# Split weights and split activations at changing byte offsets in a two-layer decoder kernel

## The chip, the cores and the metric

The kernel runs on one core of a Trainium2 chip. The time is the device time of one execution, in microseconds; the kernel before takes 2146.15 us (median of three runs, 2145.81 to 2146.16). A profile is one further execution of the same program, taken by the hardware profiler. Engines are called as the profile calls them: PE multiplies matrices (PEld is its loading of the stationary operand), DVE, ACT and POOL work elementwise, SP issues DMAs.

## The reference

Two decoder layers on 256 tokens of 2048 channels, in float32. Layer 0 mixes with a diagonal state-space model (S5) and a gated linear unit, layer 1 with windowed attention; a SwiGLU feed-forward follows each.

```python
def reference(x, ...):
    h = x
    for i in range(DEPTH):
        hn = rmsnorm(h, norm_mix[i])
        if i % N_MIXERS == 0:
            mix = s5_mixer(hn, ...)          # ends in gl = gelu(y) @ w_glu ; a * sigmoid(b)
        else:
            mix = sliding_window_attention(hn, w_qkv, b_qkv, sinks, w_o)
        h = h + mix
        hn = rmsnorm(h, norm_ffn[i])
        h = h + swiglu(hn, w_gate[i], w_up[i], w_down[i])
    return rmsnorm(h, norm_final)

def swiglu(x, w_gate, w_up, w_down):
    return (jax.nn.silu(x @ w_gate) * (x @ w_up)) @ w_down
```

Nearly all of the arithmetic is in the products with the seven weight matrices (w_glu, w_qkv, w_o, and gate, up and down twice).

## The kernel before

**Pieces.** Every weight matrix is cut into pieces of 512 rows by 512 columns, 332 in all, listed in the order of use. SP loads a piece (1 MB) into one of two `raw` buffers. ACT copies it, rounded, into the first half of a buffer `w` (L120, the high part), and DVE writes the difference `raw - high` into the second half (L121, the low part). A `w` tile is [128 partitions, 2 parts, 4 groups of channels, 512 columns], 16384 bytes on each partition.

**Three places for `w`.** `place` gives them out in turns: two buffers of the pool `wq`, allocated at the kernel's start (here: the first and the second place), and one of the pool `wp`, allocated after S5 (the third place; every third piece). While PE uses piece i, `next` has pieces up to i+2 split and up to i+4 loaded.

**Activations** are split in the same way: a tile holds [128, 2 parts, 4 groups of channels, 256 tokens], 8192 bytes on each partition. `turned_tile` (pool `pp`, four buffers) gives `gt` (the input of the gated unit), `hT` (the hidden part of SwiGLU) and `oT` (the attention's output). `normed_tile` (pool `wp`, four buffers) gives `xT`, the normalised h.

**The products.** `piece` runs 24 steps on PE for each piece of weights: 4 groups of channels, 2 halves of the tokens, and 3 products, high by high (L734), high activations by low weights (L735), low activations by high weights (L736). In each step the activations are the stationary operand (128 columns, 512 bytes on a partition, read by the weight load) and the weights the moving operand (512 columns, 2048 bytes). That makes 332 x 24 = 7968 steps. Between two pieces PE may do small work that was left for it (transposes, the attention's scores).

**Where the parts start.** Every stride inside these tiles is a multiple of 512 bytes, so that what a start address leaves modulo 512 is the same for all 24 steps of a piece. From the built program:

| tiles | pool | start modulo 512 bytes |
|---|---|---|
| `w`, first and second place | `wq` | 320 |
| `w`, third place | `wp` | 384 |
| `gt`, `hT`, `oT` | `pp` | 320 |
| `xT` | `wp` | 384 |

The *distance* of a piece is, in all that follows, the start of its activations minus the start of its weights, modulo 512 bytes. There are three distances: 0, 64 and 448. Of the 332 pieces 155 are at 0 (65 in the third place with `xT`, 46 in the second and 44 in the first place with a tile of `pp`), 131 at 64 (first or second place with `xT`) and 46 at 448 (third place with a tile of `pp`).

**Order.** The order on each engine is made by a scheduler when the program is built; instructions under `pin` or `tc.keep_in_program_order` stay where they are written. A buffer's reuse waits for the last reader of what it held.

Of the kernel before, what the change touches and what calls it, by code (L numbers as in the profile page):

```python
# [9 lines left out]
F32 = mybir.dt.float32  # L10
# [7 lines left out]
P = 128  # L18
D = 2048
# [27 lines left out]
def bc(ap, axis, n):  # L47
    """`ap` with a repeated axis of n put in."""
    v = ap.unsqueeze(axis)
    shape = list(v.shape)  # L50
    shape[axis] = n
    return v.to_broadcast(shape)
# [3 lines left out]
def kernel(  # L56
# [25 lines left out]
    # parts of activations, channels on partitions: [channel, high/low, 128 channels, token]  # L82
    def turned_tile(name):
        return pp.tile([P, 2, 4, T], F32R, tag="b8", name=nm(name))

    def normed_tile(name):
        return wp.tile([P, 2, 4, T], F32R, tag="xt", name=nm(name), bufs=4)

# [1 line left out]
    class Weights:  # L90
# [18 lines left out]
        def place(self, i):  # L109
            """in turns, but for the first the third place isn't there yet"""  # L110
            pool, n = (wp, 1) if i % 3 == 0 and i > 0 else (wq, 2)
            return pool.tile([P, 2, 4, 512], F32R, tag="w", name=nm("w"), bufs=n)
# [50 lines left out]
    # the last heads come while the first two chunks of the outputs have what the others give  # L163
# [12 lines left out]
    # work that an earlier product left for the tensor engine, done between a later one's pieces  # L176
    left = []
    # the same, a list for each of the next pieces
    slots = []

# [1 line left out]
    def s5():  # L182
        st = ExitStack()
        with st:
# [8 lines left out]
            def pin(ins):  # L193
                """in this place among its engine's work"""
                return tc.keep_in_program_order(ins)
# [7 lines left out]
            # the states; until then, room for what does not stay  # L203
# [4 lines left out]
            # loads  # L208
# [34 lines left out]
            # masks: row (j, g2, c) belongs to g2 = 0 / 1 ; sign of the re / im half  # L243
# [11 lines left out]
            def lay(nat):  # L255
                """banks of [(re/im, state), channel, group]"""
                pts = [bank([P, 4, G]) for _ in range(GC // 4)]
                for c in range(GC):
                    PE.transpose(pts[c // 4][:, c % 4], nat(c), ident)
                return pts  # L260

            def laid(pts, name, sign):
                """[(re/im, state), group, channel], times a sign per partition"""
                o = big([P, G, GC], name)
                for i, pt in enumerate(pts):
                    pin(S.activation(o[:, :, 4 * i : 4 * i + 4], pt.rearrange("p c g -> p g c"), AF.Copy, scale=sign))
                return o

            # the norm of x: rows' sums of squares
# [11 lines left out]
            # the norm's weights go into B (and D)  # L281
# [5 lines left out]
            # the other norms' weights, channels on partitions  # L287
# [4 lines left out]
            # parameters, [group, state]  # L292
# [42 lines left out]
            # powers of lambda: [group, power - 1, re/im, state]  # L335
# [5 lines left out]
            def cmul(o, a, b, n):  # L341
                """o = a * b, complex, [G, n, 2, NS]; b has one power"""
                br = bc(b[:, 0, 0], 1, n)
                bi = bc(b[:, 0, 1], 1, n)
                t = ep.tile([G, L, NS], F32, tag="cm", name=nm("cm"), bufs=2)[:, :n]
                u = ep.tile([G, L, NS], F32, tag="cm", name=nm("cm"), bufs=2)[:, :n]
                V.tensor_tensor(o[:, :, 0], a[:, :, 0], br, op=ALU.mult)
                V.tensor_tensor(t, a[:, :, 1], bi, op=ALU.mult)
                V.tensor_tensor(o[:, :, 1], a[:, :, 1], br, op=ALU.mult)
                V.tensor_tensor(u, a[:, :, 0], bi, op=ALU.mult)  # L350
                V.tensor_tensor(o[:, :, 0], o[:, :, 0], t, op=ALU.subtract)
                V.tensor_tensor(o[:, :, 1], o[:, :, 1], u, op=ALU.add)

            # q = (lambda - 1) / a ; XQ[j] = lambda^(3-j) q
# [19 lines left out]
            # the same with the state (twice) on partitions: [(2, state), power, re/im, group]  # L374
# [21 lines left out]
            # tokens: U[(j, g2, c), pair, g2' (other group's rows zero), chunk]; a quarter of the pairs  # L396
            # is eight of each half of the channels
# [24 lines left out]
            def at(pair):  # L422
                """quarter and place in it"""
                return pair % 32 // 8, pair // 32 * 8 + pair % 8
# [4 lines left out]
            # X[j] = lambda^(3-j) q B ; what each chunk adds to the states  # L429
            X = []  # L430

            def turned_x(q, b):
                px = bank([P, 4, P], "px")
                for i in range(4):
                    PE.transpose(px[:, i], X[q][:, 4 * b + i].rearrange("p j b -> p (j b)"), ident)
                xt = lp.tile([P, 4, P], F32, tag="xt", name=nm("xt"), bufs=5)
                (pin if q >= 9 else (lambda i: i))(S.copy(xt, px))
                return xt
# [16 lines left out]
            def split_groups(ap, t):  # L455
                """the quarter's groups, of an AP with groups second"""
                v = ap.rearrange("p (h g) -> p h g", h=2) if len(ap.shape) == 2 else ap.rearrange(
                    "p (h g) c -> p h g c", h=2)
                return v[:, :, 16 * t : 16 * t + 16]
# [27 lines left out]
            # states at the chunks' ends, for half of the quarters; what a chunk adds is there already  # L487
            reached = [0, 0]

            def step(hf, parts=1):  # L490
                """in as many parts as it takes to hide an operation's latency"""
                reached[hf] += 1
                k = reached[hf]
                n = 32 // parts
                ws = WS[:, :, :, 2 * hf : 2 * hf + 2].rearrange("p x r t h a -> p x r (t h a)")
                vs = []
                for i in range(parts):
                    part = slice(n * i, n * (i + 1))
                    t_ = lp.tile([P, 2, 2, n], F32, tag="sc", name=nm("sc"), bufs=4)
                    V.tensor_tensor(t_, ws[..., part], bc(Vt[hf][:, k - 1, :, part], 1, 2), op=ALU.mult)  # L500
                    vs.append((Vt[hf][:, k, :, part], t_))
                for v, t_ in vs:
                    V.tensor_tensor(v, v, t_[:, 0], op=ALU.add)  # L503
                for v, t_ in vs:
                    V.tensor_tensor(v, v, t_[:, 1, ::-1], op=ALU.add)  # L505
# [5 lines left out]
            # lambda^4 in [(g2, state), product, re/im, quarter, half, pair]  # L511
# [45 lines left out]
            # D of a chunk's channels, on the diagonal: [(lag 0, g2, c), pair, c']  # L557
# [16 lines left out]
            # K[(lag, g2, c), pair, c'], lag 3 - j, and  # L574
            # M[(j, g2, c), pair, j', c'] = K of lag j' - j
# [5 lines left out]
            def kernels(t):  # L581
# [5 lines left out]
                k = lp.tile([P, 16, 2, GC], F32, tag="xt", name=nm("k"), bufs=5)  # L587
# [15 lines left out]
            # what a chunk's own tokens give its outputs  # L603
# [22 lines left out]
            # T[(re/im, state), group, j', c'] = what a chunk's first state gives its outputs  # L626
# [12 lines left out]
            # the states laid out as each chunk's first state  # L639
# [28 lines left out]
            # the states' room goes to the first weights  # L668
# [4 lines left out]
            # outputs, gelu, channels onto partitions  # L673
# [42 lines left out]
    def rms_scale(pool, ssq, shape, keep=lambda ins: ins, between=lambda: None):  # L716
        """1 / sqrt(ssq / D + eps)"""
# [20 lines left out]
    def piece(acc, xq, first, last):  # L738
        """the next piece of the weights with 512 channels"""
# [5 lines left out]
    def linear(xt, n_pieces=None, halves=False):  # L745
        """[128 tokens, 512] x 2 in PSUM: the next pieces of the weights with the channels of xt;
        with halves, all of the first 128 tokens come before the others"""
# [19 lines left out]
    def normed(n, g):  # L767
        """channels 512 n .. of h x norm weights onto partitions (the rows' scale comes later)"""
# [12 lines left out]
    class Norm:  # L781
        """the norm of h, taken as its chunks come"""
# [6 lines left out]
        def square(self, n, t):  # L789
            junk = wp.tile([P, 512], F32, tag="junk", name=nm("junk"), bufs=2)  # L790
# [14 lines left out]
    class Last(Norm):  # L805
        """the norm of what comes out"""
# [88 lines left out]
    def attention(norm, out_norm):  # L895
        with tc.tile_pool(name="at", bufs=1) as ap:
            # minus the distance of each key, or far below where it isn't seen
# [14 lines left out]
            def bias(c):  # L912
                b = ap.tile([P, 512], F32, tag="bias", name=nm("bias"), bufs=2)
# [3 lines left out]
            # keys and values  # L917
# [21 lines left out]
            def heads(c, q):  # L939
# [44 lines left out]
                def values(g4):  # L984
# [3 lines left out]
                    def turned(i):  # L988
# [3 lines left out]
                        pT = ap.tile([P, 3, P], F32, tag="pT", name=nm("pT"), bufs=3)  # L992
# [106 lines left out]
```

## Time and profile before

| what | us |
|---|---|
| median of three runs | 2146.15 |
| span of the profiled execution, first to last instruction | 2144.7 |
| S5, until PE's first step on a piece of weights | 208.9 |
| PE busy in the span | 2044.8 |
| DVE busy | 1177.0 |
| ACT busy | 907.1 |
| POOL busy | 99.8 |

The runs' median is 1.45 us longer than the profiled span, which counts from the first instruction to the last. A row of the profile names a line of the kernel, an engine, an operation and the tiles that it writes and reads; "x332" is how many there are. A start time in a timeline is in microseconds from the span's start, with two digits. PE's matmuls are pipelined and their ends are modelled, so that the time from one start to the next says more than a matmul's own duration.

### The profile page before, as it was taken

How to read it: one execution, taken by the hardware profiler on the slowest of the kernel's cores; microseconds unless marked ns; L12 is line 12 of the kernel's file. 1: busy time of each engine (PE TensorE's matmuls, PEld its weight loads, DVE VectorE, ACT ScalarE, POOL GpSimd, SP SyncE). 2: the span in 40 equal slices, each digit the busy share in tenths (PEclk: the TensorE clock that was granted, in tenths of full speed). 3: DMA queues.
4: the chain of work that ended last, by engine and by line, in shares of the span. 5: the costliest groups of instructions: out<-in, count | busy, mean ns of one | idle time of the engine just before them, and what ended most of it. 6: DMA issues, size and time to landing. Idle time of an engine off the chain costs nothing.

```text
span 2144.7 us, 23467 instructions
## 1 busy us (share of the span) xinstructions
PE 2044.8 (95%) x9724; PEld 1674.3 (78%) x9724; DVE 1177.0 (55%) x1432; ACT 907.1 (42%) x957; POOL 99.8 (5%) x73
## 2 busy tenths in 40 slices
PE   5854999999999999999999999999999999999998
PEld 4754888888888888888888777888888888888886
DVE  8997554544444454445455776544444445444445
ACT  4737444433333333333344554443333333333333
POOL 6450100000000000000000000000000000000000
PEclk8767999999999999999999999999999999999999
DMA  4000666565555555565555433555555555655554
GB/s 120 1 21 21 226 196 193 181 194 178 190 186 193 180 193 192 180 194 180 196 177 185 143 118 119 177 184 189 178 195 189 184 190 184 196 182 191 187 187 156
DMA packets 182731, 360.53 MB, mean 168 GB/s; under 512 B 10592, under 2 KB 10656, under 8 KB 182240
## 3 DMA queue, kind: packets, MB, share of 16 engines
q1 hardware_dynamic: 181376, 355.54, 51.0%
q10 hardware_dynamic: 816, 2.16, 0.3%
q0 software_dynamic: 432, 1.33, 0.3%
q8 instruction: 76, 1.25, 0.2%
q14 instruction: 31, 0.25, 0.0%
HBM read 356.91 MB, written 2.10 MB: 167 GB/s over the span
## 4 chain that ended last, share of the span: by engine, by line
PE 88%; DVE 9%; ACT 1%; DMA 1%; issue 1%; DVEq 0%; ACTq 0%
PE acc L734 28%; PE acc L736 28%; PE acc L735 28%; DVE sc L500 2%; DVE V L503 1%; DVE V L505 1%; PE tr L855 1%; DVE X L469 1%; DVE w L121 1%; PE py L698 1%; PE tr L774 0%; DMA raw<-in_s_w_glu_dram 0%; PE po L1002 0%; ACT w L120 0%; PE tr L991 0%
## 5 line engine op out<-in xcount | busy, mean ns | idle before, releaser
L121 DVE TENSOR_TENSOR w<-raw,w 128x2048 fp32r<-128x2048 f32 x332 | 761.0, 2292 | 859.4 <-ACT w L120 859.4
L120 ACT ACTIVATE w<-raw 128x2048 fp32r<-128x2048 f32 x332 | 636.2, 1916 | 987.9 <-PE acc L736 843.9
L734 PE MATMUL acc<-w,xT 128*128 128x512 f32 x1568 | 618.7, 395 | 0.0
L735 PE MATMUL acc<-w,xT 128*128 128x512 f32 x1568 | 617.0, 393 | 0.0
L736 PE MATMUL acc<-w,xT 128*128 128x512 f32 x1568 | 617.0, 393 | 0.0
L736 PEld LDWEIGHTS acc<-w,xT 128*128 128x128 f32 x1568 | 294.0, 187 | 69.5 <-issue 1.0
L734 PEld LDWEIGHTS acc<-w,xT 128*128 128x128 f32 x1568 | 294.0, 188 | 68.9 <-issue 1.3
L735 PEld LDWEIGHTS acc<-w,xT 128*128 128x128 f32 x1568 | 294.0, 188 | 67.8 <-issue 0.5
L734 PE MATMUL acc<-w,hT 128*128 128x512 f32 x704 | 277.3, 394 | 0.0
L736 PE MATMUL acc<-w,hT 128*128 128x512 f32 x704 | 274.8, 391 | 0.0
L735 PE MATMUL acc<-w,hT 128*128 128x512 f32 x704 | 274.1, 390 | 0.0
L736 PEld LDWEIGHTS acc<-w,hT 128*128 128x128 f32 x704 | 132.2, 188 | 29.4
L734 PEld LDWEIGHTS acc<-w,hT 128*128 128x128 f32 x704 | 132.3, 188 | 28.2 <-ACT hT L857 1.2
L735 PEld LDWEIGHTS acc<-w,hT 128*128 128x128 f32 x704 | 132.3, 188 | 28.1
L735 PE MATMUL acc<-w,gt 128*128 128x512 f32 x256 | 99.9, 390 | 0.9 <-DVE w L121 0.9
L734 PE MATMUL acc<-w,gt 128*128 128x512 f32 x256 | 100.7, 394 | 0.0
L736 PE MATMUL acc<-w,gt 128*128 128x512 f32 x256 | 100.1, 391 | 0.0
L698 PE MATMUL py<-T,S 128*64 128x64 f32 x256 | 16.2, 241 | 51.5 <-DVE V L505 51.5
L882 DVE TENSOR_TENSOR h<-h,acc 128x512 f32<-128x512 f32 x64 | 43.6, 687 | 26.5 <-PE acc L736 26.5
L735 PEld LDWEIGHTS acc<-w,gt 128*128 128x128 f32 x256 | 48.1, 188 | 11.7 <-DVE w L121 1.5
L868 ACT ACTIVATE act<-acc,ry 128x512 f32<-128x512 f32 x44 | 30.2, 687 | 62.3 <-PE acc L736 62.1
L736 PEld LDWEIGHTS acc<-w,gt 128*128 128x128 f32 x256 | 48.1, 188 | 10.7
(241 smaller groups left out, 1471.0 us busy)
## 6 DMA issues: line engine op xcount, KB each, us to landing
raw<-in_ffn_w_gate_dram SPq DMA_DIRECT2D x88, 1024.0 KB, 5.2
raw<-in_ffn_w_up_dram SPq DMA_DIRECT2D x88, 1024.0 KB, 5.2
raw<-in_ffn_w_down_dram SPq DMA_DIRECT2D x88, 1024.0 KB, 5.1
raw<-in_s_w_glu_dram SPq DMA_DIRECT2D x32, 1024.0 KB, 5.3
raw<-in_attn_w_qkv_dram SPq DMA_DIRECT2D x20, 1024.0 KB, 5.1
raw<-in_attn_w_o_dram SPq DMA_DIRECT2D x16, 1024.0 KB, 5.0
xk<-in_x_dram SPq DMA_DIRECT2D x8, 256.0 KB, 7.2
h<-in_x_dram SPq DMA_DIRECT2D x2, 1024.0 KB, 7.6
```

Source lines behind the costliest of these rows:

```text
L120: keep(S.activation(hi, self.raw[i], AF.Copy))
L121: keep(V.tensor_tensor(lo, self.raw[i], hi.bitcast(F32), op=ALU.subtract))
L469: ins = eng.tensor_tensor(o[:, :, j].rearrange("p (h a) (g c) -> p h a g c", g=2, h=2), bc(split_groups(XQT[:, j, ri], t).rearrange("p h ( ...
L500: V.tensor_tensor(t_, ws[..., part], bc(Vt[hf][:, k - 1, :, part], 1, 2), op=ALU.mult)
L503: V.tensor_tensor(v, v, t_[:, 0], op=ALU.add)
L505: V.tensor_tensor(v, v, t_[:, 1, ::-1], op=ALU.add)
L698: PE.matmul(py[m][h * NK : (h + 1) * NK, i, g2], St[t][:, a, g2], Tt[q][:, 2 * pq + g2].rearrange("p a b -> p (a b)"), start=False, stop=i ...
L734: PE.matmul(acc, x_[:, 0], w[0][:, a], start=first, stop=False)
L735: PE.matmul(acc, x_[:, 0], w[1][:, a], start=False, stop=False)
L736: PE.matmul(acc, x_[:, 1], w[0][:, a], start=False, stop=last)
L868: S.activation(s, pg[t], AF.Silu, scale=r[0][:, t : t + 1])
L882: V.tensor_tensor(hc, hc, acc[t], op=ALU.add)
```

## The change

Buffers for `w` become 512 bytes longer, and so do `gt`, `hT`, `oT` and `xT`. Within its buffer a tile starts at an offset that is taken in turns from a table: 12 entries for activations, 13 for weights. The entries count elements of 4 bytes; in bytes they are 0, 64, 128, 192, 256, 320, 384, 448, 32, 16, 8, 96, and for weights also 160. To make room, four pools lose a buffer: `xt` in S5 (and its `k`) goes from 5 to 4, `junk` from 2 to 1, the attention's `bias` from 2 to 1, its `pT` from 3 to 2.

```diff
+    X_START = (0, 16, 32, 48, 64, 80, 96, 112, 8, 4, 2, 24)
+    W_START = (0, 16, 32, 48, 64, 80, 96, 112, 8, 4, 2, 24, 40)
+    turn = [0, 0]
+
+    def part(t, start, n):
+        return t[:, start : start + 8 * n].rearrange("p (r a n) -> p r a n", r=2, a=4)
+
     def turned_tile(name):
-        return pp.tile([P, 2, 4, T], F32R, tag="b8", name=nm(name))
+        turn[0] += 1
+        return part(pp.tile([P, 8 * T + 128], F32R, tag="b8", name=nm(name)), X_START[turn[0] * 5 % 12], T)
 
     def normed_tile(name):
-        return wp.tile([P, 2, 4, T], F32R, tag="xt", name=nm(name), bufs=4)
+        turn[1] += 1
+        t = wp.tile([P, 8 * T + 128], F32R, tag="xt", name=nm(name), bufs=4)
+        return part(t, X_START[(turn[1] - 1) % 12], T)
...
         def place(self, i):
             pool, n = (wp, 1) if i % 3 == 0 and i > 0 else (wq, 2)
-            return pool.tile([P, 2, 4, 512], F32R, tag="w", name=nm("w"), bufs=n)
+            return part(
+                pool.tile([P, 4096 + 128], F32R, tag="w", name=nm("w"), bufs=n), W_START[i * 5 % len(W_START)], 512
+            )
...
-                xt = lp.tile([P, 4, P], F32, tag="xt", name=nm("xt"), bufs=5)
+                xt = lp.tile([P, 4, P], F32, tag="xt", name=nm("xt"), bufs=4)
...
-                k = lp.tile([P, 16, 2, GC], F32, tag="xt", name=nm("k"), bufs=5)
+                k = lp.tile([P, 16, 2, GC], F32, tag="xt", name=nm("k"), bufs=4)
...
-            junk = wp.tile([P, 512], F32, tag="junk", name=nm("junk"), bufs=2)
+            junk = wp.tile([P, 512], F32, tag="junk", name=nm("junk"), bufs=1)
...
-                b = ap.tile([P, 512], F32, tag="bias", name=nm("bias"), bufs=2)
+                b = ap.tile([P, 512], F32, tag="bias", name=nm("bias"), bufs=1)
...
-                        pT = ap.tile([P, 3, P], F32, tag="pT", name=nm("pT"), bufs=3)
+                        pT = ap.tile([P, 3, P], F32, tag="pT", name=nm("pT"), bufs=2)
```

The buffers themselves still start at 320 or 384 modulo 512, as in the table above; the offset is added to that. The 332 pieces then lie at 55 different distances:

| distance in bytes | 0 | 1 to 63 | 64 | 65 to 255 | 256 to 447 | 448 | 449 to 511 |
|---|---|---|---|---|---|---|---|
| pieces before | 155 | 0 | 131 | 0 | 0 | 46 | 0 |
| pieces after | 18 | 37 | 19 | 97 | 112 | 22 | 27 |

In 209 of the 332 pieces the weights, the activations or both start off a multiple of 64 bytes; before, all start on one. The two operands still pass through the same buffers in the same turns, and no instruction is added or removed.

PE's and SP's instructions stand in the same order as before. On ACT and POOL the bias's buffer moves two things. On ACT, at the start of the gated unit, the scaling of the attention's first bias (`bias_883_7580`, L1026) stood between two copies of weights; before:

```order
L120 ACTIVATE w_313_1963<-raw_310_1926 128x2048
L687 CAST gt_305_1908<-pt_304_1903 128x256
L687 CAST gt_305_1908<-pt_312_1954 128x256
L120 ACTIVATE w_315_1994<-raw_311_1928 128x2048
L1026 ACTIVATE bias_883_7580<-bias_883_7580 128x512
L120 ACTIVATE w_317_2023<-raw_314_1966 128x2048
L120 ACTIVATE w_321_2054<-raw_316_1997 128x2048
```

And at the same place with the change:

```order
L134 ACTIVATE w_313_1963<-raw_310_1926 128x2048
L701 CAST gt_305_1908<-pt_304_1903 128x256
L701 CAST gt_305_1908<-pt_312_1954 128x256
L134 ACTIVATE w_315_1994<-raw_311_1928 128x2048
L134 ACTIVATE w_317_2023<-raw_314_1966 128x2048
L134 ACTIVATE w_321_2054<-raw_316_1997 128x2048
```

The scaling has left this place. On ACT, at the start of the attention, the same places between copies of weights are kept, with another chunk's bias in them; before (`bias_925_7860` is the second chunk of the queries, `bias_977_8182` the third):

```order
L120 ACTIVATE w_873_7450<-raw_862_7373 128x2048
L1026 ACTIVATE bias_925_7860<-bias_925_7860 128x512
L120 ACTIVATE w_877_7493<-raw_864_7402 128x2048
L933 COPY kT_7447<-tr_875_7479 64x4x128
L933 COPY kT_7447<-tr_876_7486 64x4x128
L120 ACTIVATE w_879_7522<-raw_874_7453 128x2048
L120 ACTIVATE w_881_7551<-raw_878_7496 128x2048
L120 ACTIVATE w_887_7588<-raw_880_7525 128x2048
L1026 ACTIVATE bias_977_8182<-bias_977_8182 128x512
L120 ACTIVATE w_901_7681<-raw_882_7554 128x2048
```

And with the change:

```order
L134 ACTIVATE w_873_7450<-raw_862_7373 128x2048
L1040 ACTIVATE bias_883_7580<-bias_883_7580 128x512
L134 ACTIVATE w_877_7493<-raw_864_7402 128x2048
L947 COPY kT_7447<-tr_875_7479 64x4x128
L947 COPY kT_7447<-tr_876_7486 64x4x128
L134 ACTIVATE w_879_7522<-raw_874_7453 128x2048
L134 ACTIVATE w_881_7551<-raw_878_7496 128x2048
L134 ACTIVATE w_887_7588<-raw_880_7525 128x2048
L1040 ACTIVATE bias_925_7860<-bias_925_7860 128x512
L134 ACTIVATE w_901_7681<-raw_882_7554 128x2048
```

Each place now holds the bias of one chunk earlier, and the last chunk's scaling takes a place further on that held none. The other moved rows are two copies of weights that pass one `junk` square, and one mask instruction of POOL that passes a bias's DMA.

## The prediction

> **What bounds the kernel now.** I read the page first (busy times, groups), then windows of the steady part, then the timeline of PE alone.
>
> ```profile
> span 2144.7 us, 23467 instructions
> PE 2044.8 (95%) x9724; PEld 1674.3 (78%) x9724; DVE 1177.0 (55%) x1432; ACT 907.1 (42%) x957; POOL 99.8 (5%) x73
> ...
> PE 88%; DVE 9%; ACT 1%; DMA 1%; issue 1%; DVEq 0%; ACTq 0%
> ...
> L121 DVE TENSOR_TENSOR w<-raw,w 128x2048 fp32r<-128x2048 f32 x332 | 761.0, 2292 | 859.4 <-ACT w L120 859.4
> L120 ACT ACTIVATE w<-raw 128x2048 fp32r<-128x2048 f32 x332 | 636.2, 1916 | 987.9 <-PE acc L736 843.9
> ```
>
> ```profile
> 600.00:800.00 200.00, 200.00 (x882) 163.22 (x881) 95.95 (x56) 74.04 (x48) 0.00 (x0) 1.00 0.58 187
> ```
>
> ```profile
> L735 PEld LDWEIGHTS acc<-w,xT x1568: 186/187/193, 388.7 to 2090.0; 128*128 128x128 f32 x196
> ...
> L734 PE MATMUL acc<-w,gt x256: 388/393/478, 208.9 to 388.1; 128*128 128x512 f32 x128
> ```
>
> ```profile
> ACT w L120 <- PE acc L736: 843.9, 247, 5.5
> ```
>
> The first fence is the page. The chain of work that ended last is PE for 88% of the span, and ACT, which feeds it, waits 843.9 us for PE to release a `w` (247 times, by the last fence, a view of who waited for whom). The second is one window of the steady part (length, then busy time of PE, PEld, DVE, ACT, POOL, then the granted clock, the DMA share, GB/s): PE has no idle time in 200 us and the granted clock is 1.00. So neither waiting nor the clock is left to gain from there; what counts is the time from one step's start to the next. Splitting costs 1.916 us on ACT and then 2.292 us on DVE, 4.21 us for a piece on which PE spends some 5.5 us, and buffers let it run two pieces ahead. The third fence, a group by tile (min/median/max ns), shows that the next step's weight load takes 187 ns: it reads while the running step still reads its moving operand. These are the two reads whose starts the change moves against each other.
>
> The timeline of PE shows whether that matters now. Rows are the first step of a piece (start, modelled duration); between two of them stand 23 more steps.
>
> ```profile
> 513.63 0.39 PE L734 MATMUL acc<-w,xT 128*128 128x512 f32 x1
> ...
> 519.09 0.39 PE L734 MATMUL acc<-w,xT 128*128 128x512 f32 x1
> ...
> 524.69 0.39 PE L734 MATMUL acc<-w,xT 128*128 128x512 f32 x1
> ...
> 598.17 0.40 PE L734 MATMUL acc<-w,hT 128*128 128x512 f32 x1
> ...
> 603.68 0.40 PE L734 MATMUL acc<-w,hT 128*128 128x512 f32 x1
> ...
> 609.17 0.39 PE L734 MATMUL acc<-w,hT 128*128 128x512 f32 x1
> ...
> 614.61 0.40 PE L734 MATMUL acc<-w,hT 128*128 128x512 f32 x1
> ```
>
> Which place a piece has follows from its number (every third is in the third place). From 513.63 to 519.09 a piece in the third place with `xT`, distance 0, takes 5.46 us; the next, in the second place, distance 64, takes 5.60. From 598.17 come the third place with `hT` (distance 448, 5.51), the second (distance 0, 5.49) and the first (distance 0, 5.44). Divided by 24, a step takes 227.5, 233.3, 229.6, 228.8 and 226.7 ns: the same engine at the same clock without idle time, 3% apart, and the order goes by the distance. The 0.02 to 0.05 us between the three pieces at distance 0 I put down to ACT's copy into another `w`, which runs in the first half of a piece.
>
> This checks against the whole: 65 x 5.46 + 131 x 5.60 + 46 x 5.51 + 46 x 5.49 + 44 x 5.44 = 1833.9 us for the 332 pieces, of the 1936 us between the first step at 208.9 (the group's first start, above) and the end; the rest is small PE work and a few waits.
>
> The Trainium skill ("SBUF — State Buffer", section "Who interferes with whom") says that only the port pair shared by VectorE and GpSimd causes contention and that PE and ACT never wait on anyone. By that rule the starts change nothing. The trace does not agree that all steps are equal, 226.7 against 233.3 ns, but it doesn't prove that the start modulo 512 is the reason; that is the third rival below.
>
> **The change, part by part.**
>
> *New distances.* Only 59 of the 332 pieces keep a distance that the trace has priced: 18 at 0, 19 at 64, 22 at 448. Together they cost 18 x 5.46 + 19 x 5.60 + 22 x 5.51 = 325.9 us. The other 273 lie where no row speaks. By the nearest rows each of them costs between 5.44 and 5.60 us: all at the lower end make 325.9 + 273 x 5.44 = 1811.0, which is 22.9 less than 1833.9; all at the upper end make 1854.7, which is 20.8 more. Gain and loss are both open. I take straight lines between the three priced distances around the circle of 512 bytes (0: 5.46, 64: 5.60, 448: 5.51), because the distance is cyclic and each unpriced one then goes by its two nearest rows. The means of the stretches are 5.53 for 1 to 63, 5.58 for 65 to 255, 5.53 for 256 to 447, 5.49 for 449 to 511. The sum: 325.9 + 37 x 5.53 + 97 x 5.58 + 112 x 5.53 + 27 x 5.49 = 1839.3 us, **5.4 us more** than before. The reason in words: distance 0, the cheapest, loses 137 of its 155 pieces, distance 64, the dearest, loses 112 of its 131, and most of the others lie on the long arc between 64 and 448, whose two ends are 5.60 and 5.51.
>
> *Starts off 64 bytes.* In 209 pieces an operand starts off a multiple of 64 bytes, which no row of before does. I put no cost of its own on that beyond the range above: the nearest rows, all on multiples of 64, are 5.44 to 5.60 apart from each other already. The same goes for ACT's and DVE's writes into `w`: were they slower, ACT's 843.9 us of waiting for PE would cover it; without that cover each 1 us would show once per piece.
>
> The Trainium skill ("TensorE: Matmul & The Clock Gate", section "Back-to-back issue gap") gives N / 2.4 + 2.5 ns for a warm matmul in isolation, an estimate of 216 ns for 512 columns; with 24 x 0.216 = 5.18 us for each of 332 pieces the sum would be 1720 us, 114 less. No piece in this trace is below 226.7 ns a step, and nothing here rests on that figure.
>
> *One bias buffer less.* The scaling at the start of the gated unit goes away:
>
> ```profile
> 232.20 0.63 ACT L1026 ACTIVATE bias<-bias 128x512 f32<-128x512 f32 x1 [8.89 <-DMA bias<-in_attn_b_qkv_dram]
> 233.88 1.92 ACT L120 ACTIVATE w<-raw 128x2048 fp32r<-128x2048 f32 x1 [1.04 <-DMA raw<-in_s_w_glu_dram]
> ...
> 1160.30 0.63 ACT L1026 ACTIVATE bias<-bias 128x512 f32<-128x512 f32 x1 [2.85 <-DMA bias<-in_attn_b_qkv_dram]
> ...
> 1183.39 0.63 ACT L1026 ACTIVATE bias<-bias 128x512 f32<-128x512 f32 x1 [2.94 <-DMA bias<-in_attn_b_qkv_dram]
> ```
>
> ```profile
> 214.00:268.00 54.00, 53.11 (x238) 43.28 (x237) 28.92 (x23) 26.11 (x27) 7.27 (x9) 1.00 0.68 224
> ```
>
> ```profile
> bias<-in_attn_b_qkv_dram POOLq DMA_DIRECT2D x5, 256.0 KB, 3.6
> ```
>
> ACT waited 8.89 us there, but the copy behind it then waited another 1.04 us for its own `raw`, so that the scaling itself was hidden; what may be gained is its transfer, 256 KB at the 224 GB/s of that window, 1.2 us earlier for the `raw` queued beside it. In the attention the two places keep their waits of 2.85 and 2.94 us on a bias that now belongs to one chunk earlier, loaded behind the same DVE release, and a fourth place gets such a wait: at most 2.9 us, in front of one copy of weights on ACT, whose average wait for PE is 843.9 / 247 = 3.4 us and covers it. So between -1.2 and +2.9; I take 0.
>
> *The other buffers.* `xt` and `k`: at most one is made ahead of the one in use, so four suffice. `junk`: ACT alone writes it, in its own order. `pT`: PE's transposes for head i+2 stand behind its products for head i. All 0, hidden by order on the same engine.
>
> Sum: +5.4. The median stands 1.45 us above the profiled span; I add the difference to the median: 2146.15 + 5.4 = **2152 us** (rounded up).
>
> **The rivals.**
>
> 1. *Most distances are free* (not slower). If only distances near 64 make the two reads meet, the unpriced 273 pieces cost 5.44: 22.9 us less, 2123 us. For it: the floor repeats exactly (226.7 ns a step in the first place with `hT`; the third place with `xT` comes to 227.5 with ACT's copy in it), so it looks like the time without a conflict. Against: 448 costs more than 0 too, so two of three distances are not free. Place: the 273 unpriced pieces. It decides from an average of (1833.9 - 325.9) / 273 = 5.52 us for these: when over half of them cost 5.44 and the rest 5.60, the kernel is faster.
>
> 2. *Only equal starts are good.* The weight load starts with its step and reads a quarter of the bytes; if it meets the moving operand's read unless both start alike, the 273 pieces cost 5.60: 20.8 us more, 2167 us. For it: both other distances are dearer than 0. Against: 448 is only half as dear as 64.
>
> 3. *The starts don't matter; the place in memory does.* First and second place and `pp` lie in the lower part of the memory, third place and `xT` in the upper, and every pairing of one distance is also a pairing of the same parts; the change keeps those. Then 2146 us, plus or minus the 3 us of the bias. The trace can't tell this from the distance. The rule of the Trainium skill above would give the same time.
>
> **How the numbers follow.** Forecast by lines 0.40, rival 1 0.26, rival 2 0.20, rival 3 0.14. A measurement of this kernel can tell about 0.2%, 4.3 us, from no change. The forecast spreads from +2 to +12, so 0.32 of it counts as slower and 0.08 as the same; rival 3 gives 0.12 the same and 0.01 on each side. Faster 0.27, same 0.20, slower 0.53. The range takes in both bounds of the unpriced pieces, rounded up by 1 at the top: 2123 to 2168.
>
> **What would show it.** In the profile after, PE should again be without idle time in the steady windows at clock 1.00, and a piece's 24 steps should take times that go with its distance, pieces at 0, 64 and 448 still 5.46, 5.60 and 5.51. Rival 1 shows as most pieces near 5.44, rival 2 as most near 5.60, rival 3 as unchanged times for each pairing of tiles. Pieces above 5.60 or below 5.44 would break the bounds, above all where a start is off a multiple of 64 bytes; so would PE idle time at the attention's start, which would be the bias.

## The result, and the profile after

The changed kernel takes 2158.60 us (median of 3 runs, 2158.30 to 2159.11) against 2146.15, a ratio of 1.0059 (95% interval 1.0039 to 1.0079): **slower, by 12.5 us**. The prediction said 2152, with 2123 to 2168 as its range. The profiled spans differ by 2157.3 - 2144.7 = 12.6 us, so the trace carries nearly all of it.

The first fence is the page of the kernel after: span, busy times, engine shares of the chain of work that ended last, and the two groups of ACT and DVE that split weights.

```profile
span 2157.3 us, 23485 instructions
...
PE 2054.8 (95%) x9724; PEld 1675.0 (78%) x9724; DVE 1177.6 (55%) x1432; ACT 908.6 (42%) x957; POOL 100.3 (5%) x73
...
PE 88%; DVE 9%; ACT 1%; issue 1%; DMA 0%; DVEq 0%; ACTq 0%; POOLq 0%
...
L135 DVE TENSOR_TENSOR w<-raw,w 128x2048 fp32r<-128x2048 f32 x332 | 761.1, 2293 | 868.2 <-ACT w L134 868.0
L134 ACT ACTIVATE w<-raw 128x2048 fp32r<-128x2048 f32 x332 | 636.1, 1916 | 1002.9 <-PE acc L750 869.5
```

The second is the window of the steady part that the prediction showed of before (length, then busy time of PE, PEld, DVE, ACT, POOL, the granted clock, DMA share, GB/s).

```profile
600.00:800.00 200.00, 200.00 (x878) 162.71 (x877) 93.70 (x55) 75.55 (x48) 0.00 (x0) 1.00 0.58 187
```

The third is the view of who waited for whom, the fourth the weight loads in the group by tile (min/median/max ns).

```profile
ACT w L134 <- PE acc L750: 869.5, 253, 5.6
```

```profile
L749 PEld LDWEIGHTS acc<-w,xT x1568: 186/188/193, 390.9 to 2102.2; 128*128 128x128 f32 x196
```

PE still has no idle time in 200 us, still at clock 1.00, but gets through 878 matmuls there instead of 882. The splitting on ACT and DVE takes 1916 and 2293 ns (1916 and 2292 before), although its results now start at 13 offsets, and a weight load takes 188 ns (187 before). ACT waits longer for PE than before, 869.5 against 843.9 us. Nothing upstream became slower: PE's steps themselves are further apart.

The timeline of PE shows six pieces in a row, by the first step of each (start, modelled duration; 23 steps between two rows).

```profile
944.34 0.39 PE L748 MATMUL acc<-w,xT 128*128 128x512 f32 x1
...
949.83 0.40 PE L748 MATMUL acc<-w,xT 128*128 128x512 f32 x1
...
955.35 0.39 PE L748 MATMUL acc<-w,xT 128*128 128x512 f32 x1
...
960.96 0.39 PE L748 MATMUL acc<-w,xT 128*128 128x512 f32 x1
...
966.45 0.39 PE L748 MATMUL acc<-w,xT 128*128 128x512 f32 x1
...
971.93 0.40 PE L748 MATMUL acc<-w,xT 128*128 128x512 f32 x1
...
977.52 0.39 PE L748 MATMUL acc<-w,hT 128*128 128x512 f32 x1
```

The six lie at distances 192, 448, 504, 0, 256 and 32 and take 5.49, 5.52, 5.61, 5.49, 5.48 and 5.59 us. Two things were not in the prediction's picture. Distance 256, in the middle of the arc that it filled with a straight line, is as cheap as 0, and 192 is as cheap as 448: distances count modulo 256. And 504 and 32, close to the cheap 0 on either side, are dear: there the weights start 8 and 32 bytes past a multiple of 64.

Grouped so, all 332 pieces of after give the table below. A step is taken from its start to the next start within the piece, without the steps of 250 ns or more, about one in a hundred (78 before, 75 after); a piece is 24 such steps.

| pieces | number | mean of a step, ns | mean of a piece, us |
|---|---|---|---|
| both starts on 64 bytes, distance 0 modulo 256 | 32 | 228.0 | 5.471 |
| both on 64, distance 64 modulo 256 | 27 | 233.3 | 5.599 |
| both on 64, distance 128 modulo 256 | 34 | 232.5 | 5.580 |
| both on 64, distance 192 modulo 256 | 31 | 229.3 | 5.503 |
| one start on 64, the other 32 bytes past it | 83 | 233.5 | 5.603 |
| both starts 32 bytes past a multiple of 64 | 16 | 231.1 | 5.546 |
| a start off a multiple of 32 | 109 | 232.2 | 5.574 |

(The last four pieces run in turns, half of the tokens at a time. Counted by their own steps, 208 pieces have a start off 64 bytes and not 209, 98 lie at 65 to 255 and 111 at 256 to 447; before, 156 lie at 0 and 45 at 448. The prediction's sums change by less than 0.1 us.)

The last three rows are the pieces with a start off 64 bytes. The 16 with both starts 32 bytes past go by their distance just as those on 64 do: 227.6 ns at 0 modulo 256 (three pieces), 233.4 at 64, 233.0 at 128, 229.1 at 192. So a start 32 bytes past a multiple of 64 is not dear in itself. The 83 with one such start lie at odd multiples of 32, and all of those distances are dear, 233.1 to 234.0 ns on average, also 32 and 224 beside the cheap 0. Where a start is off a multiple of 32, a piece takes between 226.7 and 236 ns a step; three pieces with equal starts 8 bytes past a multiple of 64 took 231.2 to 232.5. The timeline has one piece of either kind, both in the third place with `xT` at distance 0: both starts 8 bytes past (1459.74 to 1465.32, 5.58 us), then both 32 bytes past (1578.78 to 1584.23, 5.45 us).

```profile
1459.74 0.39 PE L748 MATMUL acc<-w,xT 128*128 128x512 f32 x1
...
1465.32 0.40 PE L748 MATMUL acc<-w,xT 128*128 128x512 f32 x1
...
1578.78 0.40 PE L748 MATMUL acc<-w,xT 128*128 128x512 f32 x1
...
1584.23 0.40 PE L748 MATMUL acc<-w,hT 128*128 128x512 f32 x1
```

Together the 332 pieces take 1847.9 us against 1834.2 before: **+13.7**. What is left of the span came down by 1.1 us. The timeline of ACT shows the bias in it:

```profile
233.13 1.92 ACT L134 ACTIVATE w<-raw 128x2048 fp32r<-128x2048 f32 x1 [9.06 <-DMA raw<-in_s_w_glu_dram]
...
1165.63 0.63 ACT L1040 ACTIVATE bias<-bias 128x512 f32<-128x512 f32 x1 [2.75 <-DMA bias<-in_attn_b_qkv_dram]
...
1189.53 0.63 ACT L1040 ACTIVATE bias<-bias 128x512 f32<-128x512 f32 x1 [3.38 <-DMA bias<-in_attn_b_qkv_dram]
...
1221.54 0.63 ACT L1040 ACTIVATE bias<-bias 128x512 f32<-128x512 f32 x1 [2.88 <-DMA bias<-in_attn_b_qkv_dram]
...
1259.13 0.63 ACT L1040 ACTIVATE bias<-bias 128x512 f32<-128x512 f32 x1 [3.07 <-DMA bias<-in_attn_b_qkv_dram]
```

The copy at the start of the gated unit begins at 233.13 instead of 233.88, 0.75 us earlier, and in the attention ACT waits 2.75, 3.38, 2.88 and, at the place that held none before, 3.07 us for a bias, in its own slack.

### The profile page after: what moved, and what is told of

Its sections match the earlier page's. It is cut to its first block, busy times and chain, and to the rows that moved or that the text cites. A ratio compares the mean times of both kernels' runs of the same rounds, so it can differ in the third digit from the quotient of the medians.

```text
span 2157.3 us, 23485 instructions
## 1 busy us (share of the span) xinstructions
PE 2054.8 (95%) x9724; PEld 1675.0 (78%) x9724; DVE 1177.6 (55%) x1432; ACT 908.6 (42%) x957; POOL 100.3 (5%) x73
## 4 chain that ended last, share of the span: by engine, by line
PE 88%; DVE 9%; ACT 1%; issue 1%; DMA 0%; DVEq 0%; ACTq 0%; POOLq 0%
PE acc L750 28%; PE acc L748 28%; PE acc L749 28%; DVE sc L514 2%; DVE V L519 1%; DVE V L517 1%; PE tr L869 1%; PE py L712 1%; DVE X L483 1%; ACT sc L989 1%; PE tr L788 0%; PE po L1016 0%; PE tr L1005 0%; DVE sc L977 0%; DVE w L135 0%
## 5 line engine op out<-in xcount | busy, mean ns | idle before, releaser
L135 DVE TENSOR_TENSOR w<-raw,w 128x2048 fp32r<-128x2048 f32 x332 | 761.1, 2293 | 868.2 <-ACT w L134 868.0
L134 ACT ACTIVATE w<-raw 128x2048 fp32r<-128x2048 f32 x332 | 636.1, 1916 | 1002.9 <-PE acc L750 869.5
L712 PEld LDWEIGHTS py<-T,S 128*64 128x64 f32 x256 | 16.2, 160 | 54.1 <-issue 54.1
```

What stands on the lines that cost most here:

```text
L134: keep(S.activation(hi, self.raw[i], AF.Copy))
L135: keep(V.tensor_tensor(lo, self.raw[i], hi.bitcast(F32), op=ALU.subtract))
L712: PE.matmul(py[m][h * NK : (h + 1) * NK, i, g2], St[t][:, a, g2], Tt[q][:, 2 * pq + g2].rearrange("p a b -> p (a b)"), start=False, stop=i ...
```

## The experiments

Where a letter such as A1 stands in an expectation, it is the name of a theory on what the time of a step depends on, as the expectations give them; the text after each run says what of it held. The median of the kernel before lay between 2146.21 and 2146.55 us in these runs; ratios are to it, with the 95% interval.

### The shorter pools without the offsets

```diff
-    X_START = (0, 16, 32, 48, 64, 80, 96, 112, 8, 4, 2, 24)
-    W_START = (0, 16, 32, 48, 64, 80, 96, 112, 8, 4, 2, 24, 40)
+    X_START = (0,) * 12
+    W_START = (0,) * 13
```

> The change's longer buffers and fewer buffers, all offsets 0: distances as before (155 pieces at 0, 131 at 64, 46 at 448). Theory A (the distance of the two reads, modulo 256 bytes, sets the time of a step, and nothing else of the change counts): 2146 us, within 3. Theory B (the fewer buffers carry part of the 12.5 us): 2149 to 2156 us. Rival C (the part of the memory in which the operands lie): 2146, like A.

2145.50 us, ratio 0.9996 (0.9987 to 1.0005). The longer buffers and the four pools with a buffer less cost nothing that shows; the 12.5 us come from the offsets.

### All pieces at one distance

The buffers of the third place and of `xT` start at 384 modulo 512, the others at 320. A pad of 448 bytes ahead of the former makes all alike. With the kernel before and this one line, every piece has distance 0:

```diff
     h = [wp.tile([P, D], F32, name=f"h{t}") for t in range(2)]
+    wp.tile([P, 112], F32, name="pad")
```

> The kernel before with 448 unused bytes ahead of the third place and xT, so that every piece has distance 0. Theory A: 131 pieces fall from 5.60 and 46 from 5.51 to 5.44 to 5.49 us, 332 x 5.44 to 5.47 = 1806 to 1816 against 1834 us, so 2118 to 2128 us. The lower end holds if ACT's copies disturb PE only where they write at another remainder than PE reads, the upper if they always do. Rival C: the operands stay in their parts of the memory, 2146 us.

The next two are the kernel after with that pad and one offset for all tiles: activations 64 bytes further than weights, then 256.

```diff
+    X_START = (16,) * 12
+    W_START = (0,) * 13
```

> All pieces at distance 64, with the change's buffers. Theory A: 332 x 5.60 = 1859 against 1834 us, so 2171 us, within 3. Rival C: 2146 us.

```diff
+    X_START = (64,) * 12
+    W_START = (0,) * 13
```

> All pieces at distance 256, with the change's buffers. Theory A with a period of 256 bytes, which the trace after suggests (18 pieces at 256 as cheap as those at 0): as with distance 0, 2118 to 2128 us. If the period is 512 and only equal starts are cheap (rival 2 of the prediction in full): 2167 to 2171 us.

| all pieces at | median, us | ratio | mean of a step, ns |
|---|---|---|---|
| 0 | 2120.93 | 0.9882 (0.9868 to 0.9895) | 226.8 |
| 64 | 2169.39 | 1.0107 (1.0092 to 1.0123) | 233.2 |
| 256 | 2120.42 | 0.9879 (0.9866 to 0.9893) | 226.9 |

A window of the steady part, of before and of these, shows the same at an equal clock: PE is busy for the whole 200 us each time, and only the number of matmuls differs.

```profile
1600.00:1800.00 200.00, 200.00 (x882) 163.18 (x881) 95.96 (x56) 74.97 (x48) 0.00 (x0) 1.00 0.58 189
```

```profile
1600.00:1800.00 200.00, 200.00 (x896) 165.90 (x895) 97.33 (x57) 75.66 (x48) 0.00 (x0) 1.00 0.57 192
```

```profile
1600.00:1800.00 200.00, 200.00 (x868) 161.38 (x867) 95.06 (x56) 73.72 (x47) 0.00 (x0) 1.00 0.55 186
```

```profile
1600.00:1800.00 200.00, 200.00 (x896) 165.87 (x895) 97.33 (x57) 75.66 (x48) 0.00 (x0) 1.00 0.57 191
```

From the top: before 882, all at 0 896, all at 64 868, all at 256 896. The timeline of PE, first in the kernel with all at 0, then in the one with all at 64. The rows are the first steps of the same pieces in both: one in the second place, one in the first, and the piece after them.

```profile
466.20 0.39 PE L734 MATMUL acc<-w,xT 128*128 128x512 f32 x1
...
471.64 0.39 PE L734 MATMUL acc<-w,xT 128*128 128x512 f32 x1
...
477.08 0.39 PE L734 MATMUL acc<-w,xT 128*128 128x512 f32 x1
```

```profile
471.74 0.39 PE L748 MATMUL acc<-w,xT 128*128 128x512 f32 x1
...
477.34 0.39 PE L748 MATMUL acc<-w,xT 128*128 128x512 f32 x1
...
482.94 0.39 PE L748 MATMUL acc<-w,xT 128*128 128x512 f32 x1
```

Pieces of the very same pairings of places, weights in the first or second and `xT`, take 5.44 us at distance 0 and 5.60 at 64. So the starts set the time, and the place in memory does not. 256 is as good as 0. The kernel with the pad is also **25 us under before**, with one line and no offsets; no kernel of the study beats it by more than 1.4 us.

### Both starts 8 bytes off, and a distance of 128

```diff
+    X_START = (2,) * 12
+    W_START = (2,) * 13
```

> All pieces at distance 0, but weights and activations both start 8 bytes past a multiple of 64. Theory A as so far stated (only the distance counts): 2120 us, as with all distances 0 or 256. Theory A2 (a start off 64 bytes costs by itself; the trace after has two pieces of this kind at 232.3 ns a step): 7968 x (232.3 - 226.9) = 43 us more, 2163 us.

```diff
+    X_START = (32,) * 12
+    W_START = (0,) * 13
```

> All pieces at distance 128, which no piece of the kernel before had. Straight lines between the distances known before give 5.585 us a piece, 232.7 ns a step, against 226.9 with distance 0: 7968 x 5.8 = 46 us more than 2120, 2166 us. Theory A with what the trace after shows for 128 and 384 (232.5): 2165 us. If a step depended on the distance modulo 128: 2120 us.

The first gives 2161.70 us (2159.29 to 2165.01), ratio 1.0071 (1.0056 to 1.0086), 232.1 ns a step; the second 2162.88, ratio 1.0075 (1.0059 to 1.0092), 232.5 ns. The same window of the first:

```profile
1600.00:1800.00 200.00, 200.00 (x874) 162.32 (x873) 93.71 (x56) 74.31 (x48) 0.00 (x0) 1.00 0.56 186
```

In the first, weights and activations are as far apart as in the kernel with the pad, namely not at all, yet it is 41 us slower and PE gets through 874 matmuls instead of 896. So equal starts are not enough: 8 bytes past a multiple of 64 costs by itself. This does not hold for every start off 64: the three pieces of after with equal starts 32 bytes past took 227.1 to 228.5 ns a step. The second run shows that the period is 256 bytes and not 128.

### What ACT reads

The kernel before was not even at distance 0. The timeline of PE in a piece in the second place with `hT`, every twelfth step:

```profile
603.68 0.40 PE L734 MATMUL acc<-w,hT 128*128 128x512 f32 x1
...
606.45 0.39 PE L734 MATMUL acc<-w,hT 128*128 128x512 f32 x1
...
609.17 0.39 PE L734 MATMUL acc<-w,hT 128*128 128x512 f32 x1
```

The first twelve steps take 2.77 us, the other twelve 2.72, and ACT's copy runs in the first half. In the kernel with the pad both halves take 2.72. One reading was that ACT's read of `raw` must lie at PE's remainder as well. So all weights and activations were moved 64 bytes on, which leaves `raw` at another remainder than everything that PE reads:

```diff
+    X_START = (16,) * 12
+    W_START = (16,) * 13
```

> All pieces at distance 0 with weights and activations 64 bytes further, so that PE reads and ACT and DVE write at remainder 384 while ACT and DVE read raw at 320. If what disturbed pieces at distance 0 in the first half (mean 227.7 against 226.7 ns) is ACT reading at another remainder than PE: a mean of 227.7 ns again, 7968 x 0.8 = 6 us more than all equal, 2127 us. If it is ACT writing at another remainder: 2120 us.

2119.60 us, ratio 0.9874 (0.9860 to 0.9889), with no slower half (2.73 and 2.72 us in the same piece; ACT's copy begins at 599.70):

```profile
598.38 0.39 PE L748 MATMUL acc<-w,hT 128*128 128x512 f32 x1
...
601.11 0.39 PE L748 MATMUL acc<-w,hT 128*128 128x512 f32 x1
...
603.83 0.39 PE L748 MATMUL acc<-w,hT 128*128 128x512 f32 x1
```

Where ACT reads does not matter. What is left is where it writes. Over all steps at distance 0 in the kernel before, the mean is 229.3 ns while ACT writes a `w` at another remainder than PE's operands have, and 226.9 while it writes one at the same; while DVE writes and ACT does not, it is 226.8 and 226.9. No run moved ACT's writes alone, so that they are the cause is only argued.

### Which reads meet

The prediction spoke of the next step's weight load meeting the running step's moving operand. If so, a load that reads half as much should meet it for less. In the kernel before:

```diff
-        PE.matmul(acc, x_[:, 0], w[1][:, a], start=False, stop=False)
+        PE.matmul(acc[:64], x_[:, 0, :64], w[1][:, a], start=False, stop=False)
```

> The kernel before, but the second product of each step group (L735) takes half of its stationary operand (64 of 128 columns), so that the low parts of the weights are left out for half of the tokens. Theory A as a meeting of the two reads: the step L734, during whose run that smaller load reads, loses about half of what it takes over 512 columns at full clock: at distance 64 it falls from 233 by 5 to 10 ns, at distance 0 from 227 by 0 to 7 ns; the other two steps stay. If the starts act through the step's own moving read alone, and not through the load: no step changes.

One run: 2153.02 us, 6.5 over before. The groups by tile (min/median/max ns) show that the load did become shorter:

```profile
L734 PEld LDWEIGHTS acc<-w,xT x1568: 186/188/192, 389.4 to 2096.3; 128*128 128x128 f32 x196
L735 PEld LDWEIGHTS acc<-w,xT x1568: 132/134/138, 389.6 to 2096.6; 128*64 128x64 f32 x196
```

A load of L735 takes 134 instead of 188 ns, but the fall of 5 to 10 ns did not come. At distance 64 steps keep 232.8 to 234.1 ns (233.3 before); at 0 they take 229.0 to 230.5 ns instead of 227.5 to 228.0. At 448 two of the three products came down (L734 from 232.2 to 229.6, L736 from 229.6 to 226.9) and L735 itself rose from 227.4 to 230.8. Both forms of the expectation failed: the smaller load neither shortened the steps throughout nor left them as they were.

Then one part alone was moved, from the kernel with all at distance 0 (2121 us): the low part of the activations 64 bytes further, of both operands, of the weights. The core of the edit, for the first with `n == T` around it, for the last with `n == 512`, and for both without a condition:

```diff
+            v = t[:, : 8 * n + 32].rearrange("p (r m) -> p r m", r=2)
+            return v[:, :, : 4 * n].rearrange("p r (a n) -> p r a n", a=4)
```

The lines move with the edit: the three products, in their order in the program (high by high, high activations by low weights, low activations by high weights), are the lines 748 to 750 in the expectations, 751 to 753 in the first and the last of these kernels and 749 to 751 in the second. The last expectation names the low weights' step one line too high; its number is for the low weights' product.

> All distances 0, but the low part of the activations 64 bytes further than the high part. Theory A1 (what counts is the load that reads during a step, that is the next step's activations, against this step's weights): only the step L749 (low weights, during which the low activations are loaded for L750) has distance 64, 233 ns; the other two stay at 227; mean 229 ns, 7968 / 3 x 6.5 = 17 us more than 2120, 2137 us. Theory A3 (a step's own two operands): the slow step is L750, 233 ns, and the other two 227; the same total.

> As before, but the low parts of both weights and activations 64 bytes further than the high parts. Theory A1: the load that reads during a step is at distance 0 for all three steps (high with high, low with low, high with high), so all 227 ns and 2120 us. Theory A3: L749 has low weights with high activations (distance 448, 229 ns) and L750 high weights with low activations (64, 233 ns), so 7968 / 3 x (2.3 + 6.5) = 23 us more, 2143 us.

> All distances 0, but the low part of the weights 64 bytes further than the high part; the activations' parts keep one remainder. Only the step L750 has other operands: low weights, distance 448 both to its own activations and to those loaded while it runs. If single pairs add up (A1 and A3 alike): L750 at 229 ns, the others at 227, 2120 + 2656 x 2.3 ns = 2126 us. If a step also depends on where the moving operand of the step before lay (theory A4, which would explain why both low parts together cost more than either pair does): the steps after the two changes of remainder, L750 and L751, take over 230 ns, and the time is 2135 us or more.

| low part 64 bytes further | median, us | ratio | high x high | low weights | low activations |
|---|---|---|---|---|---|
| of activations | 2151.90 | 1.0025 (1.0015 to 1.0035) | 228.5 | 229.3 | 235.4 |
| of both | 2159.54 | 1.0062 (1.0047 to 1.0077) | 230.4 | 230.9 | 234.3 |
| of weights | 2158.73 | 1.0057 (1.0040 to 1.0074) | 231.4 | 232.1 | 232.4 |

The last three columns are ns from that step's start to the next. The timeline of PE in the second of these kernels:

```profile
465.56 0.39 PE L749 MATMUL acc<-w,xT 128*128 128x512 f32 x1
465.78 0.39 PE L750 MATMUL acc<-w,xT 128*128 128x512 f32 x1
466.01 0.39 PE L751 MATMUL acc<-w,xT 128*128 128x512 f32 x1
466.24 0.40 PE L749 MATMUL acc<-w,xT 128*128 128x512 f32 x1
466.48 0.40 PE L750 MATMUL acc<-w,xT 128*128 128x512 f32 x1
466.71 0.40 PE L751 MATMUL acc<-w,xT 128*128 128x512 f32 x1
466.95 0.39 PE L749 MATMUL acc<-w,xT 128*128 128x512 f32 x1
```

Six steps make 1.39 us, and to the nanosecond they are 224, 226, 231, 236, 235 and 241: the pattern repeats after six steps, not after three, though three bring all operands back to the same starts modulo 512. The other three read the other half of the tokens, 512 bytes further, and write another accumulator. That this is not the whole reason shows in the kernel with all at 64: there the steps of nearly every piece alternate, 231 and 236 ns, across the halves of the tokens as well. In the kernel before, at the same starts modulo 512, steps at 64 took 233 or 234 ns each; two steps make 467 ns either way. Why they alternate in one kernel and not in the other stays open. With the activations' low part moved, the slow step is the one that reads it, 235.4 ns, where A3 placed it, but the other two rise as well and the total is 15 us over the 2137 expected. With both moved, 2159.5 lies above A1's 2120 and A3's 2143. With the weights' low part moved, the 2126 of A1 and A3 fails by 33 us; of the expected totals only A4's "2135 or more" holds, by which a step depends also on the remainders of the steps before it. No theory that pairs one load with one moving operand gives these three times. Whether PE's reads meet, and which, is **open**.

## Why the prediction was right in sign and short in size

**PE without idle time, so that steps set the time.** Right. The steady windows of all kernels have PE busy for the full 200 us at clock 1.00, and only the matmuls' number moves, from 868 to 896.

**The distance sets the step.** Right, and now shown rather than read off a coincidence: all at 0, 64 and 128 differ by up to 48 us with the tiles in the same places, and the shorter pools alone are worth nothing. The priced distances came back: 5.486 us at 0 (the rows at 0 said 5.44 to 5.49), 5.593 at 64, 5.505 at 448. That the next step's weight load meets the running step's moving operand, as the prediction had it, is not shown: halving a load and moving one part alone did not go by that picture. The rule of the Trainium skill ("SBUF — State Buffer", section "Who interferes with whom"), by which PE waits on no one, doesn't cover this: a step takes 226.8 or 233.2 ns by its operands' starts alone.

**The new distances, by straight lines.** The form was wrong. Distance counts modulo 256, with cheap places at 0 and 192, dear ones at 64 and 128. Yet for the 124 pieces with both starts on 64 bytes the errors cancel, by luck: the lines give 687.4 us and the trace 686.6, because 192 and 256 were costed too high and 320 and 384 too low.

**Starts off 64 bytes at no cost beyond the lines.** This is the step that failed. For the 208 pieces with such a start the lines give 1152.2 us; they took 1161.4. These 9.1 us are the whole of the 8.3 between the +13.7 of the pieces and the +5.4 of the forecast; the 124 others take 0.8 back. The loss has two parts. The 83 pieces at odd multiples of 32 took 5.603 us each, where the lines have 5.545: 4.9 us, because no priced distance lay between two multiples of 64 and the lines ran straight through, most wrongly beside the cheap 0 (5.53 for 1 to 63 and 5.49 for 449 to 511, where the trace has 5.589 and 5.563). The 109 with a start off a multiple of 32 took 4.0 us more than the lines, and the run with both starts 8 bytes past a multiple of 64 shows such a cost without any distance: 232.1 ns a step instead of 226.8. The 16 with both starts 32 bytes past are only 0.3 over the lines. The bounds of the term, 5.44 to 5.60, held its mean (5.583), though single pieces with such a start went up to 5.66.

So the sign was right in good part by luck. Before, a piece cost 5.525 us on average. Of the +13.7 us, 12.2 come from the pieces with a start off 64 bytes, of which the lines gave 3.1, and only 1.5 from those on 64, the kind of start that the priced rows have.

**ACT's and DVE's writes.** Right: 1916 and 2293 ns as before.

**One bias buffer less, and the other buffers.** Right: taken as 0 between -1.2 and +2.9; with the offsets at zero the kernel is 0.7 us under before, within the interval. The copy came 0.75 us earlier, and one wait was 3.38 us, above the 2.9 assumed, without showing in the time.

**The rivals.** *Most distances are free* named its own test: an average of 5.52 us for the 273 unpriced pieces. They average (1847.9 - 18 x 5.486 - 19 x 5.593 - 22 x 5.505) / 273 = 5.574, so it falls, although the kernels with all pieces at 0 or 256 show that its floor of 5.44 is real. Of the rivals *Only equal starts are good* is nearest in size, 2167 against 2158.6, and its 5.60 us for an unpriced piece is as near the 5.574 as the forecast's 5.54; it fails where the distance is 256 (2120 us for a kernel with nothing else) and at 192, and it has no word for equal starts that are dear. *The place in memory* is refuted: pieces with `xT` in the first and second place, 233.3 ns at 64, take 228.1 in the 13 cases on 64 bytes at 0 modulo 256 in the trace of after, and 226.8 in the kernel with the pad.

## What to carry to other kernels

Where PE is busy without a gap, compare the time from one matmul's start to the next between groups that should be equal; 3% between them can be the byte at which the operands start. Start weights and activations on a multiple of 64 bytes and at the same remainder modulo 256, if need be with a pad of a few hundred bytes; here that one line was worth 1.2%. Don't fill a gap between three measured points of an address with a straight line: a period, or what lies between the points, can cost more than the line says, and a kernel for each costs less than the guess.

## What the runs showed of the hardware

- An fp32r step of 128x512 with its own weight load takes 226.8 ns when both operands start alike modulo 256 bytes on a multiple of 64, and 233.2 ns when they start 64 apart, at the same granted clock of 1.00.
- 0 and 256 are equal (2120.93 and 2120.42 us), 128 is not (2162.88): a period of 256 bytes. Distance 192 is cheaper (229.3 ns) than 64 (233.3), so it is not symmetric around 0.
- With equal starts, both operands 8 bytes past a multiple of 64 take 232.1 ns a step; both 32 bytes past take 227.1 to 228.5 (three pieces of after), as on 64.
- With both starts on a multiple of 32, every odd multiple of 32 between them is dear: 233.1 to 234.0 ns (83 pieces of after).
- At distance 0 modulo 512, steps of the kernel before take 229.3 ns while ACT writes at another remainder modulo 512 than PE reads, 226.9 while it writes at the same, and 226.8 and 226.9 while DVE writes in its place; no run moved these writes alone.
- A load of half the width, 134 instead of 188 ns, made the kernel 6.5 us slower in its one run.
- A step's time depends on more than its own operands' starts modulo 512: with both low parts moved, the pattern repeats every six steps, with steps of 224 to 241 ns, and with all at 64 steps alternate between 231 and 236 ns.
